# Layer 0's experts add their rows to sums in DRAM by an indirect DMA, where one-hot products added them on the chip

## The chip, the core and the metric

The kernel runs on one core of one Trainium2 chip. The metric is the device time of one execution in microseconds (us): the median of three runs was 2065.11 us (2062.07 to 2066.56).

## The reference, cut to what matters

The program is a trunk of two layers over 512 latent tokens and 256 context tokens, 1024 features each. Every layer has an attention part and then a routed mixture of 16 experts. An expert picks its tokens (64 latent and, in layer 0 only, 32 context ones), and its results are added back to the rows of these tokens:

```
gates, idx = top_k(swapaxes(aff, 1, 2), cap)        # cap = 64 (latent), 32 (context)
xs = h[idx]                                         # gather
a, u = xs @ w_gate, xs @ w_up
y = (silu(a) * u) @ w_down * gates                  # per expert
out = zeros((t, d)).at[idx.reshape(-1)].add(y)      # scatter with add
x = x + m[5] * out                                  # m[5]: the gate vector of the modulation
```

A token is picked by several experts, never twice by one.

## The kernel before, in words

All in float32. The residual rows X stay in SBUF: `Xl` (four tiles of 128 latent tokens) and `Xc` (two of context tokens). `experts` (L1337 on) runs the layers' experts one after the other. Each needs 12.58 MB of weights (gate, up and down, 4 MB each), which SyncE (SP) loads in pieces of 2 MB (`load_piece`, L245) into a ring of buffers, six of them in layer 0. SP's queue waits until the piece that lay in the buffer is used up.

The loop over e issues, in this order: `gather(e+1)` on GpSimd (an indirect DMA of 96 rows out of `xn_dram`), `gate_up(e)` (L1391 latent, L1401 context), the loads of gate and up of e+1, the transposes of the gathered rows of e+1, the loads of down of e, `down(e-1)` (L1451 latent, L1464 context) and `h_transpose(e)`. Every engine works through its queue in program order.

Results are put back by one-hot products. `down` leaves a gated result in SBUF (`gated`, L1488; context L1481). After two experts `hot_lat` builds one-hot matrices from the token numbers, `scatter_lat` splits the results in two parts of reduced precision (`split`, L50 and L51) and queues eight closures in `side`, each of two matmuls (L1542, L1543) and a VectorE add to X (L1544). After four experts `hot_ctx` and `scatter_ctx` do the same for context rows (L1569 to L1571). `some(4)` inside a later `gate_up` takes four closures out of `side` after each half of the weights; `flush` runs the rest after the last expert.

Before this stands layer 0's attention, where SP loads the weights of the modulation (`ws`, L277) that TensorE multiplies between attention steps (L280).

Of the kernel before, what the change touches and what calls it, by code (L numbers as in the profile page):

```python
# [8 lines left out]
F32 = mybir.dt.float32  # L9
F32R = mybir.dt.float32r  # L10
I32 = mybir.dt.int32
U32 = mybir.dt.uint32
AF = mybir.ActivationFunctionType
OP = mybir.AluOpType
# [4 lines left out]
D = 1024  # L19
KD = 8  # L20
SEQ = 512
CTX = 256
TOK = SEQ + CTX
NLT = SEQ // 128
NT = TOK // 128
GRID_W = 64
EPS = 1e-6
NE = 16
# [15 lines left out]
class Trunk:  # L44
# [663 lines left out]
    def even_attention(self, Q, K, V, ohi, olo, pool, keep, side):  # L708
        nc = self.nc
# [58 lines left out]

        oA = Q.rearrange("p t (a d) -> p t a d", d=128)
        ssA = keep.tile([128, NT, AH], F32, name="ssA")  # L770

        def prep_A(a):
            steps = []
            for c in range(2):
                st["kA", a, c], s1 = self.k_dup(K, 2 * a + c, pool, f"kA{c}")
                st["qA", a, c], s2 = self.q_stack(Q, 2 * a + c, pool, f"qT{c}")
                steps += s1[:1] + s2[:2] + s1[1:] + s2[2:]
            return steps
# [556 lines left out]
    def experts(self, l, X, gm, sh, g5, ig, gi, wk, pieces, out=None):  # L1335
        nc, A = self.nc, self.A
        ctx = l == 0  # L1337
# [7 lines left out]
        ylat = {}  # L1345
        yctx = {}
        hot = {}

        def load_gu(e):
            self.load_pieces(l, pieces, e, GU, None)  # L1350

        def load_d(e):
            if out is not None and e == NE - 1:
                for n in range(2):
                    pieces[e, "w_exp_down", n] = self.w_columns(A["w_exp_down"], (l * NE + e) * D * D + n * 512, 2)
                return
            self.load_pieces(l, pieces, e, ("w_exp_down",))

        def gather(e):
            xs = wk.tile([96, D], F32, name="xs", tag="xs", bufs=2 if ctx else 1)  # L1360
            nc.gpsimd.indirect_dma_start(  # L1361
                out=xs[:nslot], out_offset=None, in_=self.xn_dram,
                in_offset=bass.IndirectOffsetOnAxis(ap=gi[:nslot, e:e + 1], axis=0))
            raw_xs[e] = xs
# [54 lines left out]
        def h_transpose(e):  # L1419
            h, hc = hs.pop(e)  # L1420
            pt = self.ps.tile([128, 4, 128], F32, name="pht", tag="T", bufs=4)
            for j in range(4):
                nc.tensor.transpose(pt[:, j, :], h[:, j * 128:(j + 1) * 128], self.ident)
            ht = wk.tile([128, 4, 2 * nslot], F32, name="hT", tag="hT")
            nc.scalar.activation(ht[:, :, 0:128], pt, AF.Copy)
            if ctx:
                pt2 = self.ps.tile([128, 4, 128], F32, name="pht2", tag="T", bufs=4)
                for j in range(4):
                    nc.tensor.transpose(pt2[:, j, 0:64], hc[64:128, j * 128:(j + 1) * 128], self.ident[64:128, 64:128])
                nc.vector.tensor_copy(ht[:, :, 128:192], pt2[:, :, 0:64])  # L1430
            hT[e] = ht
# [5 lines left out]

        def down(e):
            ht = hT.pop(e)
            a = e % 2  # L1440
            width = 256 if not ctx and e == NE - 2 else 512
            pl = [self.ps.tile([128, 512], F32, name="pd", tag="T", bufs=4) for _ in range(512 // width)]
            pc = self.ps.tile([128, 512], F32, name="pdc", tag="T", bufs=4) if ctx else None

            def lat(k):
                hf, j = divmod(k, 4)
                w = pieces[e, "w_exp_down", hf]
                for n in range(D // width):
                    p0 = (n + a) % 2 * 64
                    for c0 in range(0, 64, cols):  # L1450
                        nc.tensor.matmul(pl[n // 2][p0 + c0:p0 + c0 + cols, :width],  # L1451
                                         ht[:, j, hf * 64 + c0:hf * 64 + c0 + cols],
                                         w[:, j, n * width:(n + 1) * width], tile_position=tp(p0 + c0),
                                         start=(k == 0), stop=(k == KD - 1))

            cols = 32 if ctx else 64
            for k in range(KD):
                lat(k)
                if ctx:
                    hf, j = divmod(k, 4)  # L1460
                    w = pieces[e, "w_exp_down", hf]
                    for n in range(4):
                        g = (n + e) % 4
                        nc.tensor.matmul(pc[g * 32:(g + 1) * 32, :256], ht[:, j, 128 + hf * 32:160 + hf * 32],  # L1464
                                         w[:, j, n * 256:(n + 1) * 256], tile_position=tp(g * 32),
                                         start=(k == 0), stop=(k == KD - 1))
            if a == 0:
                ylat[e // 2] = [wk.tile([128, D], F32, name="yl", tag="xT", bufs=1)] + \
                    [wk.tile([128, D], F32R, name=f"yl{i}", tag=f"yl{i}", bufs=1) for i in range(2)]
            y = ylat[e // 2][0]  # L1470
            for n in range(D // width):
                gated(y, pl[n // 2], e, n, width)
            if ctx:
                if e % 4 == 0:
                    yctx[e // 4] = wk.tile([128, D], F32, name="yc", tag="yc", bufs=1)
                y = yctx[e // 4]
                for n in range(4):
                    g = (n + e) % 4
                    P = slice(g * 32, (g + 1) * 32)
                    cs = slice(n * 256, (n + 1) * 256)  # L1480
                    nc.vector.scalar_tensor_tensor(y[P, cs], pc[P, :256], ig[P, 1, 32 + e:33 + e], g5[1][P, cs],  # L1481
                                                   op0=OP.mult, op1=OP.mult)

        def gated(y, pl, e, n, width):
            g = (n + e) % 2
            P = slice(g * 64, (g + 1) * 64)
            cs = slice(n * width, (n + 1) * width)
            nc.vector.scalar_tensor_tensor(y[P, cs], pl[P, :width], ig[P, 1, e:e + 1],  # L1488
                                           g5[0][P, cs], op0=OP.mult, op1=OP.mult)
# [85 lines left out]
        def flush():  # L1575
            for f in side:
                f()
            del side[:]
# [9 lines left out]
        for e in range(NE + 1):  # L1588
            if e < NE:
                if 0 < e < NE - 1:  # L1590
                    gather(e + 1)
                gate_up(e)
                if e + 1 < NE:
                    load_gu(e + 1)
                    xs_transpose(e + 1)
                load_d(e)
            if e and e % 2 == 0:
                hot_lat(e // 2 - 1)
            if ctx and e and e % 4 == 0:
                hot_ctx(e // 4 - 1)  # L1600
            if e == NE and not ctx:
                flush()
                down_last(e - 1)
            elif e:
                down(e - 1)
                if e % 2 == 0:
                    scatter_lat(e // 2 - 1)
                if e == NE:
                    flush()
                if ctx and e % 4 == 0:  # L1610
                    scatter_ctx(e // 4 - 1)
            if e < NE:
                h_transpose(e)
        flush()


    def run(self, out):
        tc, nc, A = self.tc, self.nc, self.A
        uniq = [0]

        def pool(s, name, bufs=1, **k):
            uniq[0] += 1
            return s.enter_context(tc.tile_pool(name=f"{name}{uniq[0]}", bufs=bufs, **k))

        right = dict(side="right")
        with ExitStack() as st:
# [2 lines left out]
            self.cp = pool(st, "consts")  # L1629
            self.dr = pool(st, "dr", 1, space=DRAM)  # L1630
            self.xn_dram = self.dr.tile([TOK, D], F32, name="xn_dram")
            self.ring_i = 0
            self.later = []
            self.mrow = self.dr.tile([2, 2, 2, D], F32, name="mrow")
# [7 lines left out]
            with ExitStack() as sl:  # L1642
# [4 lines left out]
                with ExitStack() as sr:  # L1647
# [3 lines left out]
                    wk = pool(sr, "wk_first", 1, **right)  # L1651
# [71 lines left out]
                wk = pool(sl, "wk_in", 2)  # L1723
# [15 lines left out]
            op = pool(so, "o0")  # L1739
            ohi = op.tile([128, KD, TOK], F32R, name="ohi")  # L1740
            olo = op.tile([128, KD, TOK], F32R, name="olo")
            with ExitStack() as sl:
                keep = pool(sl, "keep")
                wk = pool(sl, "wk_attn", 2)
# [11 lines left out]
            X = [Xl[:, t] for t in range(NLT)] + [Xc[:, t] for t in range(NT - NLT)]  # L1756
# [5 lines left out]
            with ExitStack() as sl:  # L1762
                wk = pool(sl, "wk_out", 2)
# [16 lines left out]
            with ExitStack() as sl:  # L1780
                wk = pool(sl, "wk_moe", 2)
# [3 lines left out]
                pieces = {}  # L1785
# [5 lines left out]
                with ExitStack() as s2:  # L1791
                    tab = self.load_rope_tab(pool(s2, "tab"), A["rope32"], 32, "tab32")
                    ig, gi = self.choose(0, W, rp, wk)
# [12 lines left out]
            with ExitStack() as so:  # L1806
# [13 lines left out]
                with ExitStack() as sl:  # L1820
                    wk = pool(sl, "wk_out", 2)
# [4 lines left out]
            with ExitStack() as sl:  # L1826
                wk = pool(sl, "wk_moe", 2)
# [4 lines left out]
                pieces = {}  # L1832
# [4 lines left out]
                ig, gi = self.choose(1, W, rp, wk)  # L1837
# [43 lines left out]
```

## Time and profile before

| | us |
|---|---|
| median of the runs | 2065.11 |
| the profiled execution | 2058.84 |
| its span in the trace | 2057.1 |
| TensorE (PE) busy | 1850.6 (90%) |
| VectorE (DVE) busy | 992.6 (48%) |
| ScalarE (ACT) busy | 528.6 (26%) |
| GpSimd (POOL) busy | 282.8 (14%) |

The experts of layer 0 run from 559 us to 1144 us, those of layer 1 from about 1560 us to the end. A busy PE is not PE at its peak, and an average over the span says little: each stage has a limit of its own. DMA shares are the mean over the core's 16 DMA engines; they pass 1.00 a little where packets overlap.

### The profile page before, as it was taken

Reading aid. Unit: us, or ns where it says so; the run is one execution under the profiler, and the core shown is the slowest. Engines: PE = TensorE matmul, PEld = TensorE weight load, DVE = VectorE, ACT = ScalarE, POOL = GpSimd, SP = SyncE. Lnnn points to the kernel's source line nnn. Section 1 sums busy time; section 2 is a strip of 40 time slices with the busy share of each in tenths; the row PEclk is TensorE's granted clock in tenths of the full one; section 3 lists DMA queues with packets and bytes.
Section 4 is the critical chain, followed back from the end, with each engine's and each line's share of the span. In section 5 each row is a group of like instructions: output and inputs, shape, how many; then the busy total and the mean of one; then the engine's idle time right before and its main releaser. Section 6 shows DMA issues by size and latency. Waiting matters only on the chain.

```text
span 2057.1 us, 32103 instructions
## 1 busy us (share of the span) xinstructions
PE 1850.6 (90%) x13032; PEld 1037.0 (50%) x13032; DVE 992.6 (48%) x2333; ACT 528.6 (26%) x1204; POOL 282.8 (14%) x420
## 2 busy tenths in 40 slices
PE   7998998979699999999999778998897997888887
PEld 6877666768333333333343666676672332322224
DVE  5644878944612333324334778877553221222213
ACT  5322656742100000000000355665420000000000
POOL 2221331012200000000000034324220000000000
PEclk9999999989799999999999789999998999999999
DMA  8310333144699999999984121322278999999998
GB/s 282 92 47 23 124 101 103 63 145 164 233 374 408 362 365 357 373 357 365 377 350 173 30 65 52 96 74 68 90 272 320 398 399 399 403 397 403 397 404 323
DMA packets 149171, 505.50 MB, mean 246 GB/s; under 512 B 12559, under 2 KB 23745, under 8 KB 149025
## 3 DMA queue, kind: packets, MB, share of 16 engines
q1 hardware_dynamic: 141312, 478.84, 61.7%
q0 software_dynamic: 6752, 23.48, 3.4%
q8 instruction: 103, 1.69, 0.3%
q10 hardware_dynamic: 960, 1.14, 0.2%
q14 instruction: 44, 0.35, 0.1%
HBM read 496.06 MB, written 7.37 MB: 245 GB/s over the span
## 4 chain that ended last, share of the span: by engine, by line
PE 47%; DMA 15%; DVE 8%; ACT 2%; issue 2%; SPq 0%; POOL 0%; DVEq 0%; ACTq 0%; POOLq 0%
PE pgu L1391 15%; DMA wp<-in_w_exp_down_dram 8%; PE pd L1451 8%; DMA wp<-in_w_exp_gate_dram 6%; PE pgc L1401 5%; PE pdc L1464 3%; PE po L1245 2%; PE pg L75 2%; PE pg L76 2%; PE pg L77 2%; PE psc L1542 1%; PE pt L515 1%; PE psc L1543 1%; DMA m<-mrow 1%; PE pxs L1372 1%
## 5 line engine op out<-in xcount | busy, mean ns | idle before, releaser
L1391 PE MATMUL pgu<-wp,xsT 128*32 128x512 f32 (+1 forms) x3072 | 485.9, 603 | 31.2 <-DMA wp<-in_w_exp_gate_dram 18.4
L1391 PEld LDWEIGHTS pgu<-wp,xsT 128*32 128x32 f32 (+1 forms) x3072 | 138.3, 120 | 314.9 <-issue 279.0
L1451 PE MATMUL pd<-wp,hT 128*32 128x512 f32 (+2 forms) x1536 | 249.2, 596 | 26.2 <-DMA wp<-in_w_exp_down_dram 24.7
L1412 DVE TENSOR_TENSOR h<-pgu,h 128x512 f32<-128x512 f32 x32 | 22.0, 687 | 323.1 <-ACT h L1411 323.1
L1411 ACT ACTIVATE h<-pgu 128x512 f32<-128x512 f32 x32 | 19.1, 597 | 605.3 <-PE pgu L1391 605.3
L504 ACT ACTIVATE p<-S,nm 128x768 f32<-128x768 f32 (+1 forms) x160 | 130.6, 816 | 90.8 <-DVE nm L497 56.5
L1544 DVE TENSOR_TENSOR Xl<-psc,Xl 128x512 f32<-128x512 f32 x120 | 76.1, 685 | 160.6 <-PE psc L1543 160.6
L497 DVE TENSOR_REDUCE nm<-S 128x1 f32<-128x768 f32 (+1 forms) x160 | 134.7, 845 | 29.2 <-PE S L685 16.0
L1361 POOL DMA_INDIRECT xs<-xn_dram,gi x32 | 29.0, 908 | 843.5 <-PE pxs L1372 822.9
L1488 DVE SCALAR_TENSOR_TENSOR yl<-pd,ig,m 64x512 f32<-64x512 f32 (+1 forms) x68 | 48.8, 718 | 192.8 <-PE pd L1451 188.6
L1401 PE MATMUL pgc<-wp,xsT 128*32 128x512 f32 x1024 | 133.5, 592 | 0.0
L59 POOL TENSOR_SCALAR p<-p,sm 128x768 f32<-128x768 f32 (+1 forms) x112 | 101.0, 902 | 212.8 <-DVE sm L1224 89.2
L1451 PEld LDWEIGHTS pd<-wp,hT 128*32 128x32 f32 (+1 forms) x1536 | 69.3, 121 | 114.9 <-issue 56.2
L515 PE MATMUL pt<-ident,p 128*128 128x128 f32 x720 | 106.1, 277 | 10.0 <-DVE sm L1224 3.0
L75 PE MATMUL pg<-wi_hi,hhi 128*128 128x512 f32 (+1 forms) x240 | 89.6, 373 | 3.0 <-ACT wi_hi L50 3.0
L515 PEld LDWEIGHTS pt<-ident,p 128*128 128x128 f32 x720 | 82.5, 142 | 19.1 <-POOL q L1163 3.8
L77 PE MATMUL pg<-wi_hi,hlo 128*128 128x512 f32 (+1 forms) x240 | 89.1, 371 | 0.7 <-DVE hlo L438 0.6
L76 PE MATMUL pg<-wi_lo,hhi 128*128 128x512 f32 (+1 forms) x240 | 89.1, 371 | 0.3 <-DVE wi_lo L51 0.2
L1464 PE MATMUL pdc<-wp,hT 128*32 128x256 f32 x1024 | 78.7, 379 | 1.1 <-DVE hT L1430 1.1
L1464 PEld LDWEIGHTS pdc<-wp,hT 128*32 128x32 f32 x1024 | 33.2, 110 | 78.0 <-issue 74.7
L1401 PEld LDWEIGHTS pgc<-wp,xsT 128*32 128x32 f32 x1024 | 33.6, 110 | 76.6 <-issue 76.3
L50 ACT ACTIVATE yl<-yl 128x1024 fp32r<-128x1024 f32 (+1 forms) x17 | 17.1, 1006 | 194.0 <-DVE yl L1488 194.0
(398 smaller groups left out, 3146.3 us busy)
## 6 DMA issues: line engine op xcount, KB each, us to landing
wp<-in_w_exp_gate_dram SPq DMA_DIRECT2D x63, 2048.0 KB
wp<-in_w_exp_up_dram SPq DMA_DIRECT2D x62, 2048.0 KB
wp<-in_w_exp_down_dram SPq DMA_DIRECT2D x62, 2048.0 KB
ws<-in_w_ada_dram SPq DMA_DIRECT2D x72, 512.0 KB
ws<-in_w_ada_dram SPq DMA_DIRECT2D x8, 1024.0 KB
wi_raw<-in_w_in_even_dram SPq DMA_DIRECT2D x28, 256.0 KB
xn_dram<-xn POOLq DMA_DIRECT2D x10, 512.0 KB, 7.3
wo_raw<-in_w_out_even_dram SPq DMA_DIRECT2D x16, 256.0 KB
```

The source lines that it names most:

```text
L59: self.nc.gpsimd.tensor_scalar(out, in_, scalar, 1.0, op0=OP.mult, op1=OP.mult)
L75: mm(out, ahi, bhi, start=start, stop=False)
L76: mm(out, ahi, blo, start=False, stop=False)
L77: mm(out, alo, bhi, start=False, stop=stop)
L497: self.nc.vector.reduce_max(nm, S[:, :n], axis=AX.X, negate=True)
L504: self.nc.scalar.activation(p[:, :n], S[:, :n], AF.Exp, bias=nm, scale=1.0, accum_out=sm)
L515: nc.tensor.transpose(pt[:, j, :], p[:, (c0 + j) * 128:(c0 + j + 1) * 128], self.ident)
L1391: nc.tensor.matmul(pl[g * w:(g + 1) * w, m, :], xt[:, k, c0:c0 + w], ws(k, m, g * w // 64), tile_position=tp(g * w), **f(k))
L1401: nc.tensor.matmul(pc[g * 32:(g + 1) * 32, :], xt[:, k, 64:96], ws(k, g // 2, g % 2), tile_position=tp(g * 32), **f(k))
L1451: nc.tensor.matmul(pl[n // 2][p0 + c0:p0 + c0 + cols, :width], ht[:, j, hf * 64 + c0:hf * 64 + c0 + cols], w[:, j, n * width:(n + 1) * wid ...
L1464: nc.tensor.matmul(pc[g * 32:(g + 1) * 32, :256], ht[:, j, 128 + hf * 32:160 + hf * 32], w[:, j, n * 256:(n + 1) * 256], tile_position=tp( ...
L1544: nc.vector.tensor_tensor(X[t][:, cs], ps, X[t][:, cs], op=OP.add)
```

## The change

Layer 0 gets two tensors in DRAM, `sums`, zeroed from a tile of zeros at the start of the attention. In the experts of layer 0, latent results of experts 0 to 13 and context results of experts 0 to 11 leave `down` by `add_rows`: one VectorE operation multiplies by the gate, and an indirect DMA on GpSimd adds the tile to rows of `sums`. A token's row is cut in 2 (latent) or 4 (context) parts, one for each group of partitions, so the DMA adds 128 rows of 2 KB or of 1 KB. `load_sums` loads the sums in two buffers of the ring behind the last weights, and `add_sums` adds them to X. The last group (latent 14 and 15, context 12 to 15) keeps the one-hot products. Layer 1 is not touched.

```diff
+        zero = keep.tile([128, D], F32, name="zero")
+        nc.gpsimd.memset(zero, 0.0)
+        for t in range(NT):
+            dst = self.sums[0][t * 128:(t + 1) * 128] if t < NLT else self.sums[1][(t - NLT) * 128:(t - NLT + 1) * 128]
+            nc.sync.dma_start(dst, zero)
...
+        far = (NE - 2, NE - 4) if ctx else (0, 0)
...
+            gp = [wk.tile([128, D // n], F32, name=f"gp{n}", bufs=1) for n in (2, 4)]
+            for r, n in ((0, 2), (1, 4)):
+                for j in range(n):
+                    w = D // n
+                    nc.scalar.dma_start(gp[r][j * (128 // n):(j + 1) * (128 // n)],
+                                        self.mrow[l, 1, r:r + 1, j * w:(j + 1) * w].to_broadcast([128 // n, w]))
+        def add_rows(e, r, ps):
+            n = (2, 4)[r]
+            w = D // n
+            y = wk.tile([128, w], F32, name=f"far{r}", tag=("oh", "ohc")[r], bufs=(2, 4)[r])
+            nc.vector.scalar_tensor_tensor(y, ps[:, :w], ig[:, 1, 32 * r + e:32 * r + e + 1], gp[r],
+                                           op0=OP.mult, op1=OP.mult)
+            nc.gpsimd.indirect_dma_start(
+                out=self.sums[r].rearrange("t (n c) -> (t n) c", n=n),
+                out_offset=bass.IndirectOffsetOnAxis(ap=to[r][:, e:e + 1], axis=0), in_=y, in_offset=None,
+                compute_op=OP.add)
+        def load_sums():
+            for r, n in ((1, CTX // 128), (0, NLT)):
...
+                nc.sync.dma_start(v[:, :n], a.rearrange("(t p) c -> p t c", p=128))
+        def add_sums():
+            for r, n in ((1, CTX // 128), (0, NLT)):
+                for t in range(n):
+                    x = X[NLT * r + t]
+                    nc.vector.tensor_tensor(x, x, pieces["sums", r][:, t], op=OP.add)
...
-            if a == 0:
+            if e < far[0]:
+                add_rows(e, 0, pl[0])
+            elif a == 0:
...
-            if ctx:
+            if e < far[1]:
+                add_rows(e, 1, pc)
+            elif ctx:
...
+            if e == NE - 1 and ctx:
+                load_sums()
-            if e and e % 2 == 0:
+            if e > far[0] and e % 2 == 0:
                 hot_lat(e // 2 - 1)
...
             if e < NE:
                 h_transpose(e)
+            if e == NE - 1 and ctx:
+                add_sums()
```

On SP, where the attention of layer 0 begins, before and after (`ws`: weights of the modulation; `brow` and `mrow`: their small rows):

```order
L451 DMA wi_raw<-in_w_in_even_dram 128x512 x22
L277 DMA ws<-in_w_ada_dram 128x1024 x4
L271 DMA brow<-in_b_ada_dram 4x256 x2
L277 DMA ws<-in_w_ada_dram 128x1024 x4
L381 DMA mrow<-arow 4x256 x2
```

```order
L451 DMA wi_raw<-in_w_in_even_dram 128x512 x22
L775 DMA sums_66<-zero 128x1024 x4
L775 DMA sums_67<-zero 128x1024 x2
L277 DMA ws<-in_w_ada_dram 128x1024 x4
L271 DMA brow<-in_b_ada_dram 4x256 x2
```

Six stores of 512 KB now stand ahead of the first load of `ws`.

On VectorE, from the h of layer 0's last expert to the first adds of the last scatter, before and after (`hT`: the transposed h; `ocol` to `ohc`: the one-hot matrices; `yl` and `yc`: gated results):

```order
L1488 SCALAR_TENSOR_TENSOR yl<-pd,ig,m_5865 64x512 x2
L1481 SCALAR_TENSOR_TENSOR yc<-pdc,ig,m_5867 32x256 x4
L1430 COPY hT<-pht_9809 128x4x64
L1529 COPY ocol<-ig 64x1 x4
L1532 TENSOR_SCALAR oh<-iota,ocol 128x512 x2
L1554 COPY occ<-ig 32x1 x16
L1557 TENSOR_SCALAR ohc<-iota,occ 128x256 x4
L1488 SCALAR_TENSOR_TENSOR yl<-pd,ig,m_5865 64x512 x2
```

```order
L1480 COPY hT<-pht_9300 128x4x64
L1397 TENSOR_TENSOR Xc<-Xc,wp 128x1024 x2
L1397 TENSOR_TENSOR Xl<-Xl,wp 128x1024 x4
L1585 COPY ocol<-ig 64x1 x4
L1588 TENSOR_SCALAR oh<-iota,ocol 128x512 x2
L1610 COPY occ<-ig 32x1 x16
L1613 TENSOR_SCALAR ohc<-iota,occ 128x256 x4
L1544 SCALAR_TENSOR_TENSOR yl<-pd,ig,m_5875 64x512 x2
```

Six adds of whole tiles now stand between the last `hT` and the one-hot matrices; the last gated results come behind both.

## Rows read from the trace of the kernel before

**Rows 1.** Busy us (and count) of PE, PEld, DVE, ACT, POOL; granted clock, DMA share, GB/s.

```profile
560.00:1100.00 540.00, 538.46 (x5224) 199.78 (x5220) 177.87 (x388) 37.39 (x64) 12.10 (x14) 1.00 0.95 368
611.00:671.00 60.00, 60.00 (x592) 21.18 (x588) 15.95 (x31) 3.33 (x5) 0.90 (x1) 1.00 1.02 403
```

**Rows 2.** Groups of instructions, 560 to 1100 us: busy, mean ns, idle before.

```profile
L1391 PE MATMUL pgu<-wp,xsT 128*32 128x512 f32 x2032 | 243.3, 596 | 1.0 <-issue 1.0
L1542 PE MATMUL psc<-yl,oh 128*128 128x512 f32 x52 | 23.4, 449 | 0.0
L1569 PE MATMUL psc<-ych,ohc 128*128 128x256 f32 x24 | 7.5, 333 | 0.3
```

**Rows 3.** Waits in layer 0's experts: us in total, times, longest.

```profile
POOL xs L1361 <- PE pxs L1372: 428.3, 14, 36.4
SPq L245 <- PE pgc L1401: 345.9, 31, 22.1
```

**Rows 4.** ACT in order of time: silu of experts 1, 2, 15; two of layer 1.

```profile
604.07 0.60 ACT L1411 ACTIVATE h<-pgu 128x512 f32<-128x512 f32 x1 [21.09 <-PE pgu L1391]
637.06 0.60 ACT L1411 ACTIVATE h<-pgu 128x512 f32<-128x512 f32 x1 [19.70 <-PE pgu L1391]
...
1102.85 0.60 ACT L1411 ACTIVATE h<-pgu 128x512 f32<-128x512 f32 x1 [20.45 <-PE pgu L1391]
...
1737.89 0.60 ACT L1411 ACTIVATE h<-pgu 128x512 f32<-128x512 f32 x1 [19.11 <-PE pgu L1391]
...
1995.98 0.60 ACT L1411 ACTIVATE h<-pgu 128x512 f32<-128x512 f32 x1 [20.66 <-PE pgu L1391]
```

**Rows 5.** PE in order of time: one turn of latent closures, one of context ones.

```profile
730.76 0.50 PE L1542 MATMUL psc<-yl,oh 128*128 128x512 f32 x1
...
732.93 1.92 PE L1391 MATMUL pgu<-wp,xsT 128*32 128x512 f32 x16
...
768.08 0.38 PE L1569 MATMUL psc<-ych,ohc 128*128 128x256 f32 x1
...
769.54 1.92 PE L1391 MATMUL pgu<-wp,xsT 128*32 128x512 f32 x16
```

**Rows 6.** DMA queues (packets, MB, share of 16 engines): 1738-1996, 611-671, 2048-2057.1; gathers' landing.

```profile
q1 hardware_dynamic: 25414, 100.95, 99.5%
...
q0 software_dynamic: 222, 0.78, 4.3%
...
q10 hardware_dynamic: 576, 1.05, 31.1%
...
DMA to landing us min/median/max: 7.3/8.4/10.9
```

**Rows 7.** Start of the attention: SP, PE, a window, and POOL's 128x256 memset.

```profile
196.24 10.06 SPq L277 DMA_DIRECT2D ws<-in_w_ada_dram  x4
...
197.57 1.54 PE L633 MATMUL pt<-ident,kd 128*128 128x128 f32 x6 [4.92 <-POOL kd L59]
...
203.42 0.64 PE L280 MATMUL pa<-ws,sada 128*32 128x256 f32 x8
...
198.00:202.00 4.00, 3.74 (x16) 3.15 (x15) 1.34 (x3) 1.74 (x4) 0.00 (x0) 0.50 0.59 229
...
L161 POOL MEMSET brow<- x1: 347/347/347, 38.5 to 38.5; 128x256 f32 x1
```

**Rows 8.** End of layer 0: VectorE in order of time, its 128x1024 operation, a window.

```profile
1119.33 0.42 DVE L1430 COPY hT<-pht 128x256 f32<-128x256 f32 x1
...
1123.63 1.14 DVE L1557 TENSOR_SCALAR ohc<-iota,occ 128x256 fp32r<-128x256 f32 x4
...
1129.14 1.51 DVE L1488 SCALAR_TENSOR_TENSOR yl<-pd,ig,m 64x512 f32<-64x512 f32 x2 [4.37 <-PE pd L1451]
...
L51 DVE TENSOR_TENSOR yl<-yl,yl 128x1024 fp32r<-128x1024 f32 x7 | 8.5, 1211 | 0.1
...
1102.00:1104.00 2.00, 2.00 (x18) 0.64 (x11) 0.00 (x0) 0.89 (x2) 0.00 (x0) 1.00 0.53 213
```

More of the change, by code (lines that the diff above doesn't have):

```diff
@@ L1347, in experts @@
         hot = {}
+        far = (NE - 2, NE - 4) if ctx else (0, 0)
+        if ctx:
+            part = wk.tile([128, 4], F32, name="part", bufs=1)
+            for j in range(1, 4):
+                nc.vector.tensor_scalar(part[:, j:j + 1], self.token[:, 0:1], 32.0 * j, None, op0=OP.is_ge)
+            nc.vector.tensor_copy(part[:, 0:1], part[:, 2:3])
+            nc.vector.tensor_tensor(part[:, 1:2], part[:, 1:2], part[:, 2:3], op=OP.add)
+            nc.vector.tensor_tensor(part[:, 1:2], part[:, 1:2], part[:, 3:4], op=OP.add)
+            to = [wk.tile([128, NE], I32, name=f"to{r}", bufs=1) for r in range(2)]
+            for r in range(2):
+                nc.vector.tensor_scalar(to[r], ig[:, 0, 32 * r:32 * r + NE], (2.0, 4.0)[r], part[:, r:r + 1],
+                                        op0=OP.mult, op1=OP.add)
+            gp = [wk.tile([128, D // n], F32, name=f"gp{n}", bufs=1) for n in (2, 4)]
[4 more added lines that the diff above has]
+                                        self.mrow[l, 1, r:r + 1, j * w:(j + 1) * w].to_broadcast([128 // n, w]))
@@ new lines, in load_sums @@
+        def load_sums():
+            for r, n in ((1, CTX // 128), (0, NLT)):
+                pool = self.ring[self.ring_i % len(self.ring)]
+                self.ring_i += 1
+                v = pool.tile([128, 4, 1024], F32, name="wp", tag="w")
+                a = self.sums[r]
+                nc.sync.dma_start(v[:, :n], a.rearrange("(t p) c -> p t c", p=128))
+                pieces["sums", r] = v
+        def add_sums():
[3 more added lines that the diff above has]
+                    nc.vector.tensor_tensor(x, x, pieces["sums", r][:, t], op=OP.add)
@@ L1439, in down @@
             ht = hT.pop(e)
-            a = e % 2
+            a = e % 2 if e >= far[0] else 0
+            ac = e if e >= far[1] else 0
             width = 256 if not ctx and e == NE - 2 else 512
@@ L1462, in down @@
                     for n in range(4):
-                        g = (n + e) % 4
+                        g = (n + ac) % 4
                         nc.tensor.matmul(pc[g * 32:(g + 1) * 32, :256], ht[:, j, 128 + hf * 32:160 + hf * 32],
@@ L1466, in down @@
                                          start=(k == 0), stop=(k == KD - 1))
-            if a == 0:
+            if e < far[0]:
+                add_rows(e, 0, pl[0])
+            elif a == 0:
                 ylat[e // 2] = [wk.tile([128, D], F32, name="yl", tag="xT", bufs=1)] + \
                     [wk.tile([128, D], F32R, name=f"yl{i}", tag=f"yl{i}", bufs=1) for i in range(2)]
-            y = ylat[e // 2][0]
-            for n in range(D // width):
-                gated(y, pl[n // 2], e, n, width)
-            if ctx:
+            if e >= far[0]:
+                y = ylat[e // 2][0]
+                for n in range(D // width):
+                    gated(y, pl[n // 2], e, n, width)
+            if e < far[1]:
+                add_rows(e, 1, pc)
+            elif ctx:
                 if e % 4 == 0:
@@ L1596, in experts @@
                 load_d(e)
-            if e and e % 2 == 0:
+            if e == NE - 1 and ctx:
+                load_sums()
+            if e > far[0] and e % 2 == 0:
                 hot_lat(e // 2 - 1)
-            if ctx and e and e % 4 == 0:
+            if ctx and e > far[1] and e % 4 == 0:
                 hot_ctx(e // 4 - 1)
@@ L1605, in experts @@
                 down(e - 1)
-                if e % 2 == 0:
+                if e > far[0] and e % 2 == 0:
                     scatter_lat(e // 2 - 1)
@@ L1609, in experts @@
                     flush()
-                if ctx and e % 4 == 0:
+                if ctx and e > far[1] and e % 4 == 0:
                     scatter_ctx(e // 4 - 1)
@@ L1631, in run @@
             self.xn_dram = self.dr.tile([TOK, D], F32, name="xn_dram")
+            self.sums = [self.dr.tile([n, D], F32, name=f"sums{r}") for r, n in ((0, SEQ), (1, CTX))]
             self.ring_i = 0
```

## The prediction

> **What bounds the kernel now.** I read the page first for the shares, then the table of stretches, then layer 0's experts by lines and by waits, then ScalarE in order of time to get the step from one expert to the next, and last the DMA queues. The page's 90% for TensorE (PE) hides two different stages. In layer 0's experts PE is busy 538 of 540 us at a granted clock of 1.00, while DMA is busy 0.95 at 368 GB/s [rows 1]. The reader is to see that both are nearly full, but only one of them waits: PE's largest group has 1.0 us of idle time in the whole stage and the scatter's products none [rows 2], whereas SP waits 346 us in 31 pieces for PE to free a buffer of the ring [rows 3]. So PE sets the step here, with DMA close behind.
>
> How close, the steps tell. From the silu of expert 1 to that of expert 15 it is 1102.85 - 604.07 = 498.8 us, 14 steps of 35.63 us. The one step with no scatter in it, expert 1 to 2, takes 32.99 us [rows 4]. In layer 1, whose queue q1 alone is 99.5% of the 16 engines [rows 6] and which is therefore bound by DMA, 8 steps take 1995.98 - 1737.89 = 258.1 us, 32.26 us each [rows 4]. In layer 0 there is one stretch in which DMA is full too (share 1.02, 611 to 671 us), at 403 GB/s [rows 1]. A step there moves 12.58 MB of weights and 0.39 MB of gathered rows, 12.97 MB, which at 403 GB/s is 32.2 us. So PE without scatter needs 33.0 us, DMA without accumulates 32.2 us, and today's step is 35.6 us.
>
> **What the change removes.** In the 14 steps stand 14 turns of latent closures (730.76 to 732.93, 2.17 us each) and 6 of context ones (768.08 to 769.54, 1.46 us) [rows 5]: 30.4 + 8.8 = 39.2 us. By the steps it is 14 x (35.63 - 32.99) = 36.9 us; the difference is the ordinary handover between two groups, which stays, so I take 36.9 us. That is the most that PE can give. VectorE loses the adds to X, the splits and most one-hot matrices of these groups. It is not what is waited for, so this counts nothing; the hot matrices and the flush of the last group stay where they are.
>
> **What it adds to DMA.** Measured against 35.63 us, 14 steps of DMA have 14 x (35.63 - 32.2) = 48.0 us to spare. Against this stand 14 latent accumulates of 128 rows of 2 KB and 12 context ones of 128 rows of 1 KB, each 8 rows on each of 16 engines. No accumulate is in the trace. The nearest rows are plain transfers: in the last 9.1 us the stores of the output on q10 take 31.1% of 16 engines for 512 packets of 2 KB (64 of its 576 are tiny), 88 ns each; a packet of 4 KB of weights takes 0.995 x 16 x 258 us / 24,646 = 167 ns (the 100.95 MB by 4 KB) [rows 6]. A packet of 1 KB then is 88 - 39 = 49 ns, an estimate from these two. One transfer per row gives 14 x 8 x 88 ns + 12 x 8 x 49 ns = 14.6 us of every engine, the lower end. But an add has to read the row in DRAM besides the row in SBUF, two readings for one writing; at the price of two transfers it is 29.1 us. Rows scattered by index cost something beyond their bytes: the two gathers in 611 to 671 us hold the engines 4.3% of 60 us, 1.29 us each [rows 6], where 0.39 MB at 403 GB/s would be 0.97. These 0.32 us for each of 26 accumulates are 8 us. The upper end is an accumulate that costs what two gathers do, 2.6 us: 67 us. I take 29.1 + 8 = 37 us, the value nearest to the rows of plain packets, and keep 15 and 67 as ends.
>
> A page of the Trainium skill bears on the factor two. "Collectives: The Full Stack", section "The bandwidth ceiling: the fold count and why AG ≠ RS ≠ AR", says that an add inside the DMA engines runs at half the rate of a copy, not because of the adding but because each piece needs two source reads on the same queue. By it the sum holds 29 us, by the row of plain stores alone 15 us; no run so far shows which.
>
> So DMA has 48 - 37 = 11 us left to give, less than PE's 36.9: the step becomes one of DMA, about 34.8 us, and PE will stand idle 1.8 us in it. The rows `gp` of the gate vector (0.38 MB from DRAM, where DMA fills up) take 1 us of it: 10 us.
>
> **What it adds elsewhere.** Three places, two of which are on the path.
>
> At the start of layer 0's attention SP first has to store 3.15 MB of zeros. Today SP issues the first `ws` at 196.24 us; DMA moves it in 198 to 202 us, and PE uses it at 203.42 us without waiting [rows 7]. Now a memset comes before, four times as wide as the one of 347 ns, 1.4 us at most. The zeros then fill 7.8 us at 403 GB/s, from about 199.5 to 207, and `ws` stands behind them on the same queue: it lands at about 208.5 us. PE, which works in order, waits 5 us where nothing covers it. The memset also stands ahead of `kd` on GpSimd, for which PE waits 4.92 us today [rows 7]; it can run in this idle time, so I count 0 and keep 1.4 us for the range. I take 5 us; the lower end is 1, if the attention makes it up later.
>
> At the end of layer 0, VectorE has six adds of 128x1024 between the last `hT` and the one-hot matrices: 6 x 1.21 = 7.3 us. Today VectorE is through with these matrices at 1124.8 us and begins the last gated result at 1129.14, when PE is done: 4.4 us are free [rows 8]. So 7.3 - 4.4 = 3 us come on the path. The sums themselves are asked for when the last `gate_up` ends, since they take its buffers; DMA runs out of work then (share 0.53 in 1102 to 1104 us) [rows 8], and 3.15 MB need 7.8 us, so they are there before VectorE asks, or, with DMA as the bound, about as late as the free time allows.
>
> On GpSimd, `gather(e+2)` now queues behind the accumulates of expert e-1, which wait for VectorE's product after `down`. Today the gather is ready a step ahead: GpSimd waits up to 36.4 us in its place [rows 3]. Issued after `down`, it still has the 20 us of `gate_up` and lands in 7.3 to 10.9 us [rows 6]. I count nothing; if accumulates landed 10 us late, the transposes would wait for it.
>
> **The sum.** -10 + 5 + 3 = -2 us, with the 2% by which packet times overlap (share 1.02) -3 us. Against the profiled execution of 2058.84 us this is 2056; that execution is faster than any of the three timed ones, so I put the 3 us on their median, 2065.11: **2062 us**. A difference under 0.2%, some 4 us, can't be told from none in a measurement of this kernel.
>
> **Rivals.**
> 1. Accumulates are cheap, one transfer per row, 15 us. For it: a gather lands like any load, and nothing shows an engine held by a wait for DRAM. Against: the row in DRAM must be read. DMA would then give 48 - 15 - 1 = 32 us, still inside PE's 36.9; with 8 us for start and end it is -24: 2041 us.
> 2. Accumulates are dear: an engine holds its place in the queue while it reads, adds and writes, and the weights behind it come late. For it: a gather takes a third more engine time than its bytes. Against: that is little. It decides from 48 - 1 - 8 = 39 us in all, 1.5 us for each accumulate; at the upper end of 67 us the sum is -48 + 67 + 1 + 8 = +28: 2093 us. PE would wait for weights in every step, at a step of 37 us.
> 3. The gain comes as forecast, but start and end cost more: PE's clock, 0.50 in 198 to 202 us after an idle time [rows 7], falls again in the new wait, and the sums come late. Twice 8 us instead of 8: +5, 2070 us.
>
> The Trainium skill has a rule that makes for rival 2. "DMA: Bandwidth & Descriptors", section "Anatomy of one DMA — SWDGE (gpsimd) path", puts a fixed cost of about 2.0 us on every DMA of GpSimd besides its bytes. Taken as engine time, 26 x 2.0 + 15 = 67 us. By the gather's row only 0.32 us beyond the bytes show as time of the engines, so most of that fixed part must be latency, which is hidden here; the rule is one more way to rival 2's time, and no likelier than the rows make it.
>
> **How the numbers follow.** The forecast has 0.45, with a range of its own of 2051 to 2072 (accumulates from 25 to 46 us). Rival 1 has 0.2, rival 2 0.25, rival 3 0.1. Faster by over 0.2% are rival 1 and somewhat under half of the forecast: 0.42. Within 0.2%: a third of the forecast and half of rival 3: 0.21. Slower: rival 2, the rest of rival 3 and of the forecast: 0.37. The range goes from rival 1 to just past rival 2's price, 2040 to 2095.
>
> **What would show it.** Right: steps of 34 to 35.5 us in layer 0, DMA share at 1.0 throughout, PE idle for 1 to 2 us per step with a DMA of `wp` named as the releaser, SP's waits for PE much shorter than 346 us; PE waiting some 5 us for `ws` at 203 us; VectorE beginning the last gated result some 3 us after PE is done. Steps of 33 us with no idle PE would mean cheap accumulates; steps over 36 us, or GpSimd waiting for its own accumulates, dear ones. The forecast is wrong altogether if a step is longer than today's, or if the attention makes up for the wait or doubles it.

## The result, and the profile after

The changed kernel takes 2049.11 us (median of 4 runs, 2048.21 to 2050.27) against 2065.84 us of the kernel before (4 runs beside it, 2062.07 to 2067.1): a ratio of 0.9922, 95% interval 0.9905 to 0.994. It is faster by 16.7 us where 3 were forecast. The time lies inside the whole range, 2040 to 2095, but 2 us below the range that the forecast gave itself, 2051 to 2072, and above the 2041 of rival 1. The two profiled executions differ by less, 2048.65 against 2058.84 us, 10.2 us, because that execution of before is faster than its median. The ledger below compares those two traces: where each stands in time, in us from the start of its span.

| place | before | after | after less before |
|---|---|---|---|
| `kd` transposes, attention | 197.57 | 199.81 | +2.2 |
| first product on `ws` | 203.42 | 211.32 | +7.9 |
| silu of expert 1 | 604.07 | 617.36 | +13.3 |
| silu of expert 15 | 1102.85 | 1087.93 | -14.9 |
| last gated result on VectorE | 1129.14 | 1115.21 | -13.9 |
| end of the span | 2057.1 | 2046.8 | -10.3 |

So the kernel arrives at the experts 13.3 us late, wins 28.2 us in 14 steps, loses 1 us at the end of layer 0 (up to the last gated result), and loses 3.6 us from there to the end, mostly in layer 1, whose code is the same. (From the router's last exp in layer 1 to the end it is 514.2 us before and 516.9 after, and 514.0 to 517.0 in the other versions below, so those 3.6 us are mostly scatter. The 2.2 us at the `kd` transposes are for the most part scatter too: a new memset takes 0.6 of them, and in three other versions, with that memset, these transposes begin anywhere from 196.8 to 199.4 us.)

**The steps.** Against the steps in [rows 4], these are the silus of experts 1, 2, 7, 8, 14 and 15, ScalarE in order of time: start in us, duration, operation, and in brackets the idle time before it.

```profile
617.36 0.60 ACT L1461 ACTIVATE h<-pgu 128x512 f32<-128x512 f32 x1 [21.08 <-PE pgu L1441]
650.35 0.60 ACT L1461 ACTIVATE h<-pgu 128x512 f32<-128x512 f32 x1 [19.70 <-PE pgu L1441]
...
815.85 0.60 ACT L1461 ACTIVATE h<-pgu 128x512 f32<-128x512 f32 x1 [20.22 <-PE pgu L1441]
851.18 0.60 ACT L1461 ACTIVATE h<-pgu 128x512 f32<-128x512 f32 x1 [21.99 <-PE pgu L1441]
...
1054.94 0.60 ACT L1461 ACTIVATE h<-pgu 128x512 f32<-128x512 f32 x1 [20.40 <-PE pgu L1441]
1087.93 0.60 ACT L1461 ACTIVATE h<-pgu 128x512 f32<-128x512 f32 x1 [19.64 <-PE pgu L1441]
```

From 617.36 to 1087.93 it is 470.6 us, 33.61 us a step where it was 35.63. The steps are not alike: the first six take (815.85 - 617.36) / 6 = 33.08 us on the mean, nearly the 32.99 of the step without scatter, the next seven (1054.94 - 815.85) / 7 = 34.16 (single ones from 32.98 to 35.33), and the last is 32.99 again. The windows show the turn (stretch, its length, then PE, PEld, DVE, ACT and POOL busy, the granted clock, the DMA share, GB/s); they answer to [rows 1].

```profile
600.00:1080.00 480.00, 472.45 (x4800) 166.31 (x4796) 74.19 (x132) 24.95 (x42) 52.90 (x39) 1.00 1.03 394
825.00:1055.00 230.00, 222.82 (x2252) 77.18 (x2248) 33.56 (x60) 11.35 (x20) 26.87 (x20) 1.00 1.03 397
```

DMA's share has risen from 0.95 to 1.03. PE has been idle for 480 - 472.45 = 7.6 us, and 230 - 222.82 = 7.2 of them lie between 825 and 1055 us. The groups of waits of the experts say for what (total us, times, longest us), the counterpart of [rows 3]:

```profile
PE pgu L1441 <- DMA wp<-in_w_exp_up_dram: 7.5, 6, 2.1
PEld pgu L1441 <- DMA wp<-in_w_exp_up_dram: 13.0, 6, 3.0
...
POOL sums L1379 <- DVE far L1377: 435.2, 14, 56.5
...
SPq L245 <- PE pgc L1451: 305.7, 31, 19.5
```

PE now waits for weights, six times. GpSimd waits as long as before, but for VectorE's product ahead of the accumulate. SP's wait for PE, 305.7 us, is only a little shorter than its 345.9 us before.

**The attention's start** (SP, then PE, in order of time, and windows as above), beside [rows 7]:

```profile
199.21 5.36 SPq L775 DMA_DIRECT2D sums<-zero  x6
204.61 10.77 SPq L277 DMA_DIRECT2D ws<-in_w_ada_dram  x4
```

```profile
199.81 1.54 PE L633 MATMUL pt<-ident,kd 128*128 128x128 f32 x6 [5.49 <-POOL kd L59]
...
211.32 1.08 PE L280 MATMUL pa<-ws,sada 128*32 128x256 f32 x8 [6.74 <-DMA ws<-in_w_ada_dram]
```

```profile
206.00:210.00 4.00, 0.00 (x0) 0.00 (x0) 0.09 (x1) 0.78 (x2) 1.38 (x2) 0.97 1.00 330
210.00:214.00 4.00, 2.68 (x16) 1.36 (x20) 0.42 (x1) 0.00 (x0) 0.00 (x0) 0.50 0.46 141
214.00:218.00 4.00, 4.00 (x26) 3.00 (x27) 3.21 (x7) 1.65 (x4) 1.40 (x2) 0.67 0.64 223
```

SP's first `ws` comes 8.4 us later than at 196.24. PE does nothing from 206 to 210 us while the DMA engines are full (zeros, then `ws`), and when it starts again the granted clock is 0.50, the lower of its two levels (1.2 GHz), then 0.67 on the mean. In the kernel before the clock is low from 198 to 206 us (0.50, then 0.84) and 1.00 from 206 to 218. The changed kernel has that stretch too (0.69 in 198 to 202 us), so this is a second one.

**The end of layer 0** (VectorE in order of time), beside [rows 8]:

```profile
1102.55 2.36 DVE L1397 TENSOR_TENSOR Xc<-Xc,wp 128x1024 f32<-128x1024 f32 x2
1105.67 4.63 DVE L1397 TENSOR_TENSOR Xl<-Xl,wp 128x1024 f32<-128x1024 f32 x4 [0.76 <-DMA wp<-sums]
...
1114.06 1.14 DVE L1613 TENSOR_SCALAR ohc<-iota,occ 128x256 fp32r<-128x256 f32 x4
1115.21 1.51 DVE L1544 SCALAR_TENSOR_TENSOR yl<-pd,ig,m 64x512 f32<-64x512 f32 x2
```

Six adds of 7.0 us stand ahead of the one-hot matrices, and the sums land 0.76 us after VectorE asks for the latent ones. The last gated result waits for PE's last latent products of `down` (PE in order of time):

```profile
1110.77 1.04 PE L1502 MATMUL pd<-wp,hT 128*32 128x512 f32 x8
```

They end at 1111.81 us, and VectorE begins the result at 1115.21, 3.4 us later, where in the kernel before it was 0.1 us. The ledger shows a loss of only 1 us, because PE is there sooner: in the kernel before, a turn of latent closures stood behind the last silu (1102.85 us), and it is gone. PE before, in order of time:

```profile
1103.57 0.50 PE L1542 MATMUL psc<-yl,oh 128*128 128x512 f32 x1
...
1105.75 1.06 PE L1451 MATMUL pd<-wp,hT 128*32 128x512 f32 x8
```

### The profile page after: what moved, and what is told of

It is laid out like the page before. It is cut to its first block, busy times and chain, and to the rows that moved or that the text cites. A ratio compares the mean times of both kernels' runs of the same rounds, so it can differ in the third digit from the quotient of the medians.

```text
span 2046.8 us, 31615 instructions
## 1 busy us (share of the span) xinstructions
PE 1819.0 (89%) x12872; PEld 1013.9 (50%) x12872; DVE 899.4 (44%) x2096; ACT 517.1 (25%) x1185; POOL 324.2 (16%) x447
## 5 line engine op out<-in xcount | busy, mean ns | idle before, releaser
L1379 POOL DMA_INDIRECT sums<-far,to x26 | 40.7, 1564 | 438.8 <-DVE far L1377 435.2
L1475 ACT ACTIVATE hT<-pht 128x512 f32<-128x512 f32 x32 | 19.0, 593 | 240.1 <-PE pht L1473 240.1
L1544 DVE SCALAR_TENSOR_TENSOR yl<-pd,ig,m 64x512 f32<-64x512 f32 (+1 forms) x40 | 27.9, 696 | 114.2 <-PE pd L1502 110.2
L1451 PEld LDWEIGHTS pgc<-wp,xsT 128*32 128x32 f32 x1024 | 33.6, 110 | 76.7 <-issue 76.4
```

Source lines behind the costliest of these rows:

```text
L1379: nc.gpsimd.indirect_dma_start(out=self.sums[r].rearrange("t (n c) -> (t n) c", n=n), out_offset=bass.IndirectOffsetOnAxis(ap=to[r][:, e:e ...
L1451: nc.tensor.matmul(pc[g * 32:(g + 1) * 32, :], xt[:, k, 64:96], ws(k, g // 2, g % 2), tile_position=tp(g * 32), **f(k))
```

## Experiments

The first question was what an accumulate costs; the lead theory was two transfers per row (29 us in all), the rival one that accumulates are cheap and something else holds the steps at 33.6 us. Each ratio is to the kernel before as timed beside that version: 2066.7 us for the first four (7 runs), 2061.58 us for the last four (14 runs). Since these differ by 5 us, versions of the two groups are compared by their ratios or by stretches of their traces. The changed kernel's ratio is 0.9922 [0.9905, 0.994].

**The zeros stored later.** The six stores of `zero` are wrapped in a function and issued after the attention's modulation products:

```
                     pass
+                self.clear_sums()
                 gm, sh = res[0, 4], res[0, 3]
```

> The six stores of zeros are issued by SP behind the last load of the attention, not ahead of the first; nothing else changes. Theory: TensorE's wait for the first modulation weights (6.7 us in the changed kernel) and the low clock behind it go, and since weights of layer 0's experts and TensorE both start earlier by that much, all of it reaches the end: about 7 us less than the changed kernel's 2049, 2042. Rival: the attention makes up for the wait later, or the weights of the experts come no earlier: within 2 us of 2049.

Measured: 2041.71 us (4 runs, 2037.99 to 2045.48), ratio 0.9886 [0.9851, 0.9921]. In its trace PE in order of time begins on `ws` without a wait:

```profile
204.26 0.64 PE L280 MATMUL pa<-ws,sada 128*32 128x256 f32 x8
```

From the `kd` transposes to the choice of tokens (the product `pi`) it is 352.6 us, as in the kernel before (352.3), where the changed kernel has 360.4: the place of the zeros costs 7.8 us there. At the silu of expert 15 5.2 of them are left (882.9 us from the `kd` transposes instead of 888.1). The ratio alone hardly tells this version from the changed kernel, since the intervals meet. The 14 steps stay at 471.4 us.

**No accumulate, and a plain one.** Two runs: one leaves the indirect DMA out, so the far experts' results are lost; the other leaves only the add out, so that rows overwrite each other:

```
-            nc.gpsimd.indirect_dma_start(out=..., in_=y, in_offset=None, compute_op=OP.add)
```

```
-                in_=y, in_offset=None, compute_op=OP.add)
+                in_=y, in_offset=None)
```

> The 26 accumulating DMAs are left out (the experts' rows but for the last groups don't reach the output); VectorE's products, zeros, loads and adds of the sums stay. Theory (DMA's engines are the limit from the eighth expert on, before that a full ring covers it): all 14 steps at TensorE's 33.0 us, 462 us from expert 1 to 15 against 470.6, no wait for weights, 2040. Rival (the waits for weights come from the uneven load of single DMA engines or from SP's order, not from the accumulates): some of the waits stay, 466 us or more, 2045.

> The 26 DMAs write their rows without adding (so a token keeps only one expert's row). Theory: what costs is the second read, so packets of 2 KB take 88 ns and not the 176 ns of the changed kernel; DMA's step is then 32.2 + 1.05 = 33.2 us, which the ring's lead covers: 462 us, time as without them, about 2041. Rival (a row scattered by index costs the same, added or not): packets of 176 ns, 470 us, 2049.

Measured: 2036.9 us (2 runs), ratio 0.9864 [0.9824, 0.9904], and 2040.42 us (2 runs), ratio 0.9881 [0.9841, 0.9922]. In both the 14 steps take 461.82 us, 33.0 each, and PE is busy without a gap. The windows of the one without a DMA and of the one with the plain DMA (columns as above):

```profile
620.00:1080.00 460.00, 460.00 (x4690) 162.07 (x4692) 73.57 (x131) 23.90 (x41) 10.83 (x12) 1.00 1.01 393
```

```profile
620.00:1080.00 460.00, 460.00 (x4692) 162.44 (x4688) 74.25 (x132) 25.08 (x42) 37.73 (x39) 1.00 1.02 405
```

The plain DMA writes the same rows to the same places, at 405 GB/s in all, and PE never waits. So what binds the changed kernel is what the add costs beyond writing the rows by index over this queue. The DMA queue of GpSimd (packets, MB, share of 16 engines) sizes it: 616 to 1086 us of the changed kernel, 616 to 1076 us without accumulates, and with plain ones.

```profile
q0 software_dynamic: 5200, 10.36, 9.7%
```

```profile
q0 software_dynamic: 1344, 4.72, 3.4%
```

```profile
q0 software_dynamic: 3152, 10.36, 6.3%
```

Without accumulates 12 gathers hold each engine for 3.4% of 460 us, 1.30 us each. The other two stretches have 13 gathers, 16.9 us; what is left for the 26 accumulates is 45.6 - 16.9 = 28.7 us, and for 26 plain ones 29.0 - 16.9 = 12.1 us. In the records of single packets a 2 KB row of an accumulate lasts 176 ns, twice the 88 ns of a 2 KB row stored by q10 in the kernel before. The plain scatter is no such pair: its records are packets of 4 KB. The counts above show it (5200 - 3152 = 2048 fewer, which is 1792 rows of 2 KB and 1536 of 1 KB less the 1280 packets of 4 KB that hold the same bytes), and so does the line on sizes from 616 to 1076 us, with none between 512 bytes and 2 KB:

```profile
DMA packets 47340, 186.33 MB, mean 405 GB/s; under 512 B 1962, under 2 KB 1962, under 8 KB 47300
```

So an accumulate costs 2.0 times a store row by row, and 28.7 / 12.1 = 2.4 times the plain scatter of the same bytes.

**The accumulate twice, into the same sums.** The indirect DMA is issued a second time, which doubles what is added:

```
+            nc.gpsimd.indirect_dma_start(out=self.sums[r]..., in_=y, in_offset=None, compute_op=OP.add)
```

> Each accumulating DMA is issued twice (the sums get twice the rows). Theory: DMA's step grows from 34.2 to 36.2 us, and DMA is the limit nearly from the start: 14 x 36.2 less a lead of about 9 us, some 498 us from expert 1 to 15 against 470.6, time about 2077. Rival (accumulates cost DMA's engines little, and the late steps wait for something else): under 480 us, under 2060.

Measured: 2188.64 us (2 runs, 2187.09 and 2190.2), ratio 1.0599 [1.0555, 1.0643], over 110 us above what either theory gave. Both were wrong on this kernel. Its waits (total us, times, longest us) and a window tell why:

```profile
POOL sums L1383 <- DMA sums<-far,to: 198.6, 25, 9.3
...
PE pxs L1426 <- DMA xs<-xn_dram,gi: 123.7, 12, 11.8
```

```profile
700.00:1100.00 400.00, 309.05 (x2972) 108.09 (x2976) 44.54 (x80) 14.85 (x25) 62.65 (x44) 0.88 0.87 304
```

The DMA engines are at 0.87, not full. The second accumulate writes the tensor of the first, so in this program GpSimd's queue waits some 8 us for the first to land, 25 times; the next expert's gather stands behind it in the same order, and PE waits for the gather, 10 us in each of 12 steps. This run can't give the price of an accumulate on the DMA engines, but it prices a dependent one.

**The accumulate twice, into sums of its own.** So it was done again with the late zeros and a second set of sums:

```
+            nc.gpsimd.indirect_dma_start(out=self.sums2[r]..., in_=y, in_offset=None, compute_op=OP.add)
```

> As with the zeros late, but every accumulate is issued a second time into a second pair of tensors (also zeroed late), so that none waits for the one before it, which the first try at doubling did not avoid. Theory: DMA's step is 32.2 + 2 x 2.0 = 36.2 us, 14 of them less a lead of 9 us are 498 us from expert 1 to 15 against 471 with single ones; time about 2069. Rival (accumulates cost DMA's engines little; the first try was slow only by its waits): under 480 us, under 2052.

Measured: 2070.15 us (7 runs, 2064.04 to 2071.96), ratio 1.0032 [1.0017, 1.0047], and 500.1 us for the 14 steps, 28.7 more than with the late zeros alone: 26 accumulates more cost their 29 us in full, as the theory had it (498 us; the rival under 480). Its waits and a window:

```profile
PE pgu L1450 <- DMA wp<-in_w_exp_up_dram: 26.8, 11, 5.4
```

```profile
600.00:1080.00 480.00, 453.03 (x4492) 156.00 (x4488) 68.57 (x122) 24.43 (x41) 90.11 (x63) 0.98 1.03 380
```

PE's wait for weights has grown from 7.5 to 26.8 us, with the DMA share at the same 1.03, and the whole gain over the kernel before is gone.

**The gate vector's rows copied on the chip.** The `gp` DMAs out of DRAM are replaced by copies on ScalarE:

```
-                    nc.scalar.dma_start(gp[r][...], self.mrow[l, 1, r:r + 1, ...].to_broadcast(...))
+                    nc.scalar.activation(gp[r][P], g5[r][P, j * w:(j + 1) * w], AF.Copy)
```

> Of the changed kernel only the six DMAs of the gate rows go (0.38 MB, in flight beside the first gather); ScalarE copies these rows from the tile that is loaded anyway. Theory (from the first weights on DMA is the limit, and a later start of TensorE only fills the ring): the first gather lands 3 us earlier and expert 1's silu comes 3 us earlier, but expert 15's at most 1 us earlier; about 2048. Rival (TensorE's start counts in full): 3 us at both, 2046.

Measured: 2044.47 us (4 runs, 2042.09 to 2048.3), ratio 0.9919 [0.9899, 0.9938]. The time does not tell the two apart; the trace does. PE in order of time at the first gathered rows:

```profile
563.88 0.88 PE L1422 MATMUL pxs<-ident,xs 96*128 96x96 f32 x4 [5.54 <-ACT gp L1371]
```

In the changed kernel this wait is 8.62 us, before it 5.71. From `pi` to the silu of expert 1 it is 54.6 us instead of 57.2, 2.6 earlier, but to that of expert 15 it is 526.9 instead of 527.7: of 2.6 us only 0.9 are left at the end. In this pair an earlier start is hardly handed on, as it should be if DMA sets when the last steps run. But the same edit is also in the last version below, and against the late zeros alone it gives 54.5 us instead of 58.9 to expert 1 and 525.7 instead of 530.3 to expert 15: all of it is handed on. So these traces do not settle what an earlier start is worth; the 14 steps of the versions with single accumulates differ by 1.7 us among themselves (470.6 to 472.2).

**Accumulates for the latent half alone.** With the late zeros, the context tokens go back to one-hot products:

```
-        far = (NE - 2, NE - 4) if ctx else (0, 0)
+        far = (NE - 2, 0) if ctx else (0, 0)
```

> As with the zeros late, but the context rows of all experts keep one-hot products; only latent rows go by accumulates, and only their sums are loaded. Theory: DMA's step falls by 12 x 0.8 / 14 / 1.03 = 0.7 us to 33.5, TensorE's grows by 6 turns of 1.46 us to 33.6; both limits meet and the 14 steps take 471 us as with all rows, time within 2 us of 2042. Rival (TensorE and DMA slow each other down when both are full): 474 us or more, 2046.

Measured: 2040.94 us (4 runs, 2039.83 to 2042.23), ratio 0.9897 [0.988, 0.9915], 470.5 us for the steps. Window:

```profile
600.00:1080.00 480.00, 479.72 (x4844) 172.57 (x4840) 114.80 (x264) 29.71 (x54) 34.80 (x27) 1.00 1.02 392
```

PE is busy 479.7 of 480 us and still takes the same time: it waits no more, but has the context products to do (462 + 8.8 = 471). The balance has tipped back to PE at no gain.

**All that cost something, mended.** Late zeros, gate vector copied, and the last group's one-hot matrices built before the adds instead of behind them:

```
                 load_sums()
+                hot_lat(NE // 2 - 1)
+                hot_ctx(NE // 4 - 1)
```

> The zeros behind the attention's last weights, the gate rows by copies, and the last group's one-hot matrices built before the sums are added, in VectorE's idle time under the last products of expert 14. Theory: 7 us from the zeros, 1 from the gate rows, and the 3 us by which VectorE begins the last gated result late: 2038. Rival: the end is set by the sums, which come no earlier: 2041.

Measured: 2032.68 us (5 runs, 2027.5 to 2038.41), ratio 0.9859 [0.9837, 0.9882], faster than both kernels. It is below both times that were expected, but those were reckoned from the changed kernel's 2049; by the ratios it is 0.0063 x 2066 = 13 us ahead of the changed kernel, where 11 were expected. VectorE in order of time at the end of layer 0:

```profile
1095.80 4.63 DVE L1400 TENSOR_TENSOR Xl<-Xl,wp 128x1024 f32<-128x1024 f32 x4 [1.03 <-DMA wp<-sums]
...
1101.76 1.51 DVE L1547 SCALAR_TENSOR_TENSOR yl<-pd,ig,m 64x512 f32<-64x512 f32 x2 [1.33 <-PE pd L1505]
```

VectorE now waits 1.33 us for PE where PE's result waited 3.4 us for VectorE. From the silu of expert 15 to the last product of the scatter it is 38.1 us instead of 41.9 (40.9 in the kernel before). The 14 steps stay at 471.2 us.

## Why the prediction was right and wrong

The direction, the limit and the places of the costs were right; the size of the gain was not. That the time lies inside the range says little, since the range reached from cheap accumulates to dear ones, and no case that was named stood at 2049. Some luck is in it too: the steps gave 17 us more than was put, and 4 us of that are hidden, since outside the steps the change cost 8.1 (from `kd` to `pi`) + 0.6 (memset) + 3.0 (`gp`) + 1.0 (end) = 12.7 us where 5 + 1 + 3 = 9 were put. Together that is 28.2 - 12.7 = 15.5 us, near the gain by the medians.

**What bounds it: right.** PE set the steps; with the scatter's products gone its own step is 33.0 us (both runs without the add), and DMA became the limit: share 1.03, and waits that name `wp`. Three signs were off in size. The mean step is 33.61 us, below the 34 to 35.5 that were named (only seven of the 14 average 34.16). PE's idle time is 7.6 us in the stage, about 0.5 a step and not 1.8. SP's wait for PE hardly shrank (305.7 us of 345.9), so that it was no sign for which of two near limits binds.

**What the change removes: 36.9 us right, the reason for it wrong.** Fourteen turns of latent closures were counted in the steps, and the 2.3 us by which turns (39.2) and steps (36.9) differ were called the ordinary handover between groups, which stays. But [rows 2] have 52 products of L1542 up to 1100 us, 13 turns, and the fourteenth stands at 1103.57 us, behind the last silu. 13 x 2.17 + 6 x 1.46 = 37.0 us is what the steps show, so no handover is left over; the fourteenth turn, 2.2 us, is a gain at the end of layer 0 that the sum does not have.

**The price of an add: right in its largest part.** Two transfers per row were put at 29.1 us; the queue's share gives 28.7, and a second set of accumulates added 28.7 us to the steps. The section of "Collectives: The Full Stack" on the fold count, in the Trainium skill, has half the rate of a copy for the adding step of a collective, and gives two source reads as the reason. The trace agrees with the size: 176 ns for a row against 88 ns. That the second transfer is the read of the row in DRAM, and not the adding, no run here shows.

**The sum: this is the step that failed.** "So DMA has 48 - 37 = 11 us left to give": measured are 28.2 us in the steps, 17 more. Two of its terms are mis-sized.
- The 0.32 us for "rows scattered by index", 8 us in all, taken over from the gathers, are not there: 28.7 us is the price of two transfers and nothing more. The plain scatter, at 12.1 us, even lies below the 14.6 of one transfer per row, since it goes in packets of 4 KB.
- The 48 us count all 14 steps as if DMA had to keep up from the first. At two transfers DMA's step is 32.2 + 29.1 / 14 = 34.3 us, and the seven steps from expert 7 to 14 show 34.16. But the first six ran at 33.08, near PE's own pace, while DMA was already full (share 1.03 from 616 to 782 us). 14 x 34.3 = 480 us against 470.6: some 9.6 us, of which the first six steps give 6 x (34.3 - 33.08) = 7.3 and the last one 1.3. That this is a lead of buffers already loaded is not shown directly, but the run with accumulates apart shows nearly the same lead with dearer steps: at 32.2 + 58.2 / 14 = 36.4 us a step 14 of them are 509 us, against 500.1 measured, and there the lead is used up after two steps (32.99 us each, the third 35.5). The expectation of that run had used this lead, 9 us, beforehand and came to 498 us. The size of the lead was not varied by itself, and the two pairs with the gate vector's copies disagree on it.

**The start: mechanism right, size off.** The wait for `ws` was put at 5 us and is 6.74; with the low clock behind the wait it is 7.8 us up to `pi`, by the run that moves the zeros. The memset, which that run leaves in its place, adds 0.6 us (PE's wait for `kd` is 5.49 us instead of 4.92) where 0 to 1.4 were put. The clock is what rival 3 spoke of: 0.50 and 0.67 in 210 to 218 us. The `gp` rows were put at 1 us; they hold up the first gather by 3 us (8.62 instead of 5.71 us), and how much of that reaches the end is open.

**The end: cause right, net cost smaller.** VectorE was forecast to be 3 us late and begins the last gated result 3.4 us after PE is done; building the matrices first takes it back. But the net loss is 1.0 us, since the fourteenth turn of closures, 2.2 us, is no longer ahead of PE's last products. The sums came 0.76 us after they were asked for, as "about as late as the free time allows".

**GpSimd's queue: right.** Accumulates land in 8.7 us (median) and gathers in 9.8 instead of 8.4, and PE never waited for a gather in the steps. A gather issued at 633.94 us, so landed at about 644, is used at 651.08: some 7 us are to spare. The run with dependent accumulates shows what stands behind this: two landings one after the other ahead of the gather give steps of about 45 us.

**Rival 2's rule.** "DMA: Bandwidth & Descriptors" of the Trainium skill, in its section on the SWDGE path, has a fixed 2.0 us for each DMA of GpSimd. The same section puts most of it down to the wait until the last byte is confirmed in the target memory, so by the page itself it is latency, as the prediction judged, and not time of the engines. The runs agree: 28.7 us / 26 = 1.1 us of the engines for a whole accumulate, against 8.7 us to its landing.

**Still open.** By the medians the gain is 16.7 us, by the two traces 10.2. Some 5 of the 6.5 us between them stand in stretches that the change does not touch: 3.6 behind layer 0's last gated result and 1.6 ahead of the `kd` transposes (2.2 less the memset's 0.6). All runs of the kernel before go from 2058 to 2069 us; what makes these stretches scatter was not settled.

## What to carry to other kernels

Price an accumulating DMA at two transfers of each of its rows (here 176 ns for 2 KB, against 88 ns stored) and set that against what the engine it relieves can give; where both limits are near, the gain ends at the nearer one, and buffers already loaded may push the point where the other limit bites several steps back. Count also the work that the change takes away behind the last step. Look at what a one-time preparation stands ahead of in its queue: 3 MB of zeros cost 7.8 us in front of a load that PE was waiting for, and 0.3 us at most, by the same stretch, when they were stored behind the last of these loads, at 381.6 us. Two accumulates into the same tensor one behind the other, ahead of a gather, cost 12 us a step here (45 us instead of 33).

## What was not expected of the hardware

- An accumulate's packets hardly vary in the records: 176 ns for a 2 KB row and 101 ns for a 1 KB row, at a DMA share of 1.03 as at 0.87, while gathered rows of 4 KB average 199 ns and packets of weights 163 ns.
- The plain scatter of the same rows shows packets of 4 KB, so that leaving out the add saves more than half: 12.1 us of the engines instead of 28.7.
- Issuing an accumulate holds GpSimd for 1.56 us, the same DMA without the add for 0.98 us. From the page of the changed kernel, then of the one with the plain DMA (instructions | busy us, mean ns of one | idle time before them):

```profile
L1379 POOL DMA_INDIRECT sums<-far,to x26 | 40.7, 1564 | 438.8 <-DVE far L1377 435.2
```

```profile
L1379 POOL DMA_INDIRECT sums<-far,to x26 | 25.6, 984 | 445.1 <-DVE far L1377 441.4
```

- In this program an accumulate into a tensor that another is still adding to is held back until that one has landed: 7.9 us on the mean, up to 9.3, on the issuing engine.
